# Encoder of two layers on one core: seven up-projection chunks a layer by seven products, with low parts of neighbouring weights made by DMA

## The chip, the core and the metric

The kernel runs on one core of a Trainium2 chip. The core has a matrix engine (TensorE, PE in the profile; PEld are its weight loads), a vector engine (VectorE, DVE), an activation engine (ScalarE, ACT), GpSimd (POOL) and SyncE (SP). Each runs its own stream of instructions in order and waits for the others by semaphores. DMA transfers are issued by one of these engines and then run on 16 DMA engines. The metric is the device time of one execution in microseconds; less is better.

## The reference

What must be computed, for 512 tokens (`S`) of 1024 features (`D_MODEL`), all in float32, for two layers (a gated linear attention mixer in layer 0, softmax attention in layer 1):

```python
for i in range(DEPTH):
    h = rmsnorm(x, norm_mix[i])
    x = x + (gla_mixer(h, ...) if i % 2 == 0 else attn_mixer(h, ...))
    x = x + conv_ffn(rmsnorm(x, norm_ffn[i]), ffn_w_up[i], ffn_w_conv[i], ffn_b_conv[i], ffn_w_down[i])

def conv_ffn(h, w_up, w_conv, b_conv, w_down):
    u = h @ w_up                          # 512 x 1024 by 1024 x 5632
    u = depthwise convolution of width 3 along the tokens, + b_conv
    val, gate = jnp.split(u, 2, axis=-1)
    return (jax.nn.silu(gate) * val) @ w_down     # 512 x 2816 by 2816 x 1024
```

The change concerns `h @ w_up` in both layers.

## The kernel before

**Products of float32.** A float32 matrix is held as a high part (`wh`, rounded to the matrix engine's format fp32r) and a low part (`wl`, what the rounding left). One product is three matmuls: high by high (L361), high by low (L362), low by high (L363).

**Chunks.** The up projection of a layer has 22 chunks m, 0 to 21. A chunk is 128 features of the value and 128 of the gate. A plain chunk (`plain_up`) is two halves t = 0 and 1, each of 8 blocks of 128 input features by three matmuls of 512 columns: 24 matmuls a half, 48 a chunk. The results get the norm's factor in L804 (DVE), then the convolution (`act_up`: L859 on ACT, L860 and L861 on DVE, for each half), the activation (L863, ACT) and the product of the two (L864, DVE). Two finished chunks are made into operands of the down projection by `prepare`, with `split` (L870 ACT, L871 DVE).

**Chunks by seven products.** For a chunk in the list `SEVEN`, `seven_up` multiplies blocks of two by two in the manner of Strassen and Winograd: seven products of sums of blocks in place of eight. Each is 12 matmuls of 256 columns (L816), 84 a chunk. The sums of input blocks are made once a layer, those of weights for every such chunk, by `summed`: L158, L159, L166, L172 add on DVE; the high parts are made on ACT (L162 twice, L174, L183, L187); the low parts on DVE (L163 twice, L175, L188), except the low part of the piece h = 2: there ACT writes minus the high part into the low tile (L184, a copy with scale −1, rounded as the high part is) and a DMA on POOL's queue adds the raw weights to it (L194), which leaves the low part. The piece h = 1 lies in a tile of its own, `ring`, of which there is one. The products come in the order 1, 6, 7, 2, 5, 4, 3. Product 1 is begun between the halves of the chunk before it (the `begun` list). ACT copies partial results between banks (L827 after product 1, L831 after product 6, which product 4 adds to; L841, L842, L845), and DVE finishes them (L836, L843 to L849).

**Down projection.** Right after the first half of chunks 9 and 17 `down_part` begins one of two parts of the down projection, by seven products too, in four rows of outputs; its copies on ACT are L930, L939 and L945. What the parts leave is done plainly at the end of the layer.

**Weights.** A strip is the 1 MB of weights of one chunk, loaded by SP's queue (L136) into `raw`, of which there are two buffers. A buffer is free for the next strip when everything that reads the last one is done: for a plain chunk that is both halves' high and low parts. The halves are split into `wh` and `wl`, three buffers of each. For a plain half that is one copy on ACT (L204) and one subtraction on DVE (L205), both of 1024 elements a partition. Matrices in the list `by_dma` (some of the attention's) are done in the other way: two copies on ACT (L144 into `wh`, L145 negated into `wl`) and the accumulating DMA (L194) on POOL's queue.

**The order.** Nothing plans the order but the program text: `W.todo` lists halves and pieces in the order in which they are used, `W.half` or `W.piece` first issues the DMAs that are pending (`flush`), makes what is asked for if it isn't made, and then makes more from the list until as many are made ahead as its last argument says. That argument is 1 for a plain half and 2 to 5 near a chunk by seven products or a down part, by the table `ahead`; for pieces it is 3.

Of the kernel before, what the change touches and what calls it, by code (L numbers as in the profile page):

```python
# [45 lines left out]
DOWN_AFTER = {9: 0, 17: 1}  # L46


SEVEN = (5, 12, 19, 21)


PC_NORM = 0
# [7 lines left out]
def hybrid_encoder_kernel(  # L60
# [54 lines left out]
    class Weights:  # L115
# [2 lines left out]

        def __init__(self):
            self.todo, self.made, self.raw, self.by_dma, self.pending = [], {}, {}, [], []  # L120
            self.sums, self.last, self.fine = set(), None, []

        def add(self, src, strips=None, pieces=2):
            for i in strips or range(src.shape[0]):
# [4 lines left out]
        def make(self, key):  # L129
            src, i, h = key  # L130
            if h == 0 and (id(src), i) not in self.raw:
                t = sp.tile([P, 4 * S], F32, tag="raw", bufs=2, name=nm("raw"))
                n = 4 if any(src is a and i < m for a, m in self.fine) else 1
                for q in range(n):
                    sl = slice(q * 4 * S // n, (q + 1) * 4 * S // n)
                    sync.dma_start(t[:, sl], src[i, :, sl])  # L136
                self.raw[id(src), i] = t
            if (id(src), i) in self.sums:
                self.made[id(src), i, h] = self.summed(self.raw[id(src), i], h)
                return  # L140
            r = self.raw[id(src), i][:, h * 2 * S : (h + 1) * 2 * S]
            hi, lo = pair("wh", 3, F32R, "wh"), pair("wl", 3, F32R, "wl")
            if any(src is a and i < n for a, n in self.by_dma):
                act.activation(hi, r, AF.Copy)  # L144
                act.activation(lo, r, AF.Copy, scale=-1.0)  # L145
                self.pending.append((lo, r))
            else:
                self.split(hi, lo, r, 2 if src is w_vg and i < 2 else 1, src is w_vg and i == 0 and h == 0)
            self.made[id(src), i, h] = (hi, lo)
# [73 lines left out]
    W = Weights()  # L223
# [8 lines left out]

    def add_ffn(layer):
        first = 0
        for m, part in DOWN_AFTER.items():
            add_up(layer, range(first, m + 1))
            W.add(down_w[layer], range(part * NQ, (part + 1) * NQ), 4)
# [136 lines left out]
    def feature_tile(*a):  # L374
        for last in feature_steps(*a):
            pass
        return last
# [396 lines left out]
    def ffn(layer, norm, cw, nxt):  # L774
# [10 lines left out]
        def plain_up(m):  # L785

            pss = []
            for t in range(2):
                ps = bank("s" if t else "acc", "up")
                feature_tile(*W.half(up[layer], 2 * m + t, ahead.get((m, t), 1)), norm.hl, ps)  # L790
                pss.append(ps)
                if t == 0 and m + 1 in SEVEN:
                    begun.append(seven_up(m + 1))
# [531 lines left out]
```

## Time and profile before

| What | us |
| --- | --- |
| Median of three runs (1109.46, 1110.05, 1112.25) | 1110.05 |
| The profiled execution's own time | 1110.01 |
| Its span | 1108.3 |
| PE busy | 1099.6 (99%) |
| DVE busy | 852.9 (77%) |
| ACT busy | 614.8 (55%) |
| POOL busy | 94.5 (9%) |
| The feed-forward stage of layer 0 within the span | about 225 to 560 |

The profile is of one execution. Busy time of an engine is time in which one of its instructions ran. "Idle before" and the releaser say how long an engine stood still before an instruction and which instruction ended that. Matmuls are pipelined, so the time from start to start says what one costs, and the ends are modelled. Starts are in us from the span's start. The plain chunks of layer 0 fall, for example, into 243.20 to 264.96 (two chunks); the four chunks by seven products end at 291.35, 406.91, 522.89 and 543.87.

### The profile page before, as it was taken

Reading aid. Unit: us, or ns where it says so; the run is one execution under the profiler, and the core shown is the slowest. Engines: PE = TensorE matmul, PEld = TensorE weight load, DVE = VectorE, ACT = ScalarE, POOL = GpSimd, SP = SyncE. Lnnn points to the kernel's source line nnn. Section 1 sums busy time; section 2 is a strip of 40 time slices with the busy share of each in tenths; the row PEclk is TensorE's granted clock in tenths of the full one; section 3 lists DMA queues with packets and bytes.
Section 4 is the critical chain, followed back from the end, with each engine's and each line's share of the span. In section 5 each row is a group of like instructions: output and inputs, shape, how many; then the busy total and the mean of one; then the engine's idle time right before and its main releaser. Section 6 shows DMA issues by size and latency. Waiting matters only on the chain.

```text
span 1108.3 us, 15700 instructions
## 1 busy us (share of the span) xinstructions
PE 1099.6 (99%) x6068; PEld 956.3 (86%) x6068; DVE 852.9 (77%) x1401; ACT 614.8 (55%) x998; POOL 94.5 (9%) x102
## 2 busy tenths in 40 slices
PE   9999999999999999999999999999999999999998
PEld 7888888888889988898888888788888998889887
DVE  6785785679998878976965578766999887897693
ACT  5565343456656554654664777645665655465460
POOL 0100122000000000000004243000000000000000
PEclk9999999999999999999999999999999999999999
DMA  6422222222426343353447765422151634335342
GB/s 231 141 88 97 75 96 76 77 77 92 156 67 179 98 133 114 107 160 95 145 139 187 173 182 154 161 77 81 72 171 47 179 118 133 114 98 156 109 134 76
DMA packets 32571, 134.78 MB, mean 122 GB/s; under 512 B 3952, under 2 KB 4464, under 8 KB 22128
## 3 DMA queue, kind: packets, MB, share of 16 engines
q1 hardware_dynamic: 21072, 102.16, 26.5%
q0 software_dynamic: 6528, 23.07, 10.6%
q10 hardware_dynamic: 4896, 8.55, 2.1%
q8 instruction: 47, 0.77, 0.3%
q14 instruction: 28, 0.23, 0.1%
HBM read 100.21 MB, written 2.10 MB: 92 GB/s over the span
## 4 chain that ended last, share of the span: by engine, by line
PE 93%; DVE 4%; ACT 1%; DMA 1%; issue 0%; POOL 0%; ACTq 0%; SPq 0%; DVEq 0%
PE r L816 21%; PE up L361 11%; PE up L362 11%; PE up L363 11%; PE vg L393 8%; PE op L419 8%; PE dn L362 2%; PE dn L363 2%; PE dn L361 2%; PE o L687 1%; PE A L361 1%; PE av L393 1%; PE A L363 1%; PE A L362 1%; PE pt L1184 1%; PE q L361 1%
## 5 line engine op out<-in xcount | busy, mean ns | idle before, releaser
L361 PE MATMUL up<-xhl,wh 128*128 128x512 f32 x576 | 224.8, 390 | 0.0
L362 PE MATMUL up<-xhl,wh 128*128 128x512 f32 x576 | 224.4, 390 | 0.0
L363 PE MATMUL up<-xhl,wl 128*128 128x512 f32 x576 | 224.2, 389 | 0.0
L204 ACT ACTIVATE wh<-raw 128x1024 fp32r<-128x1024 f32 x116 | 122.6, 1057 | 142.2 <-PE up L362 58.4
L205 DVE TENSOR_TENSOR wl<-raw,wh 128x1024 fp32r<-128x1024 f32 x116 | 141.5, 1220 | 31.7 <-ACT wh L204 31.4
L363 PEld LDWEIGHTS up<-xhl,wl 128*128 128x128 f32 x576 | 108.1, 188 | 22.6
L361 PEld LDWEIGHTS up<-xhl,wh 128*128 128x128 f32 x576 | 108.2, 188 | 21.8
L362 PEld LDWEIGHTS up<-xhl,wh 128*128 128x128 f32 x576 | 108.2, 188 | 21.6
L816 PE MATMUL r<-gu,wh 128*128 128x256 f32 x640 | 116.6, 283 | 0.6 <-ACT r L945 0.6
L816 PEld LDWEIGHTS r<-gu,wh 128*128 128x128 f32 x640 | 99.7, 191 | 1.3 <-ACT r L945 1.0
L194 POOL DMA_DIRECT2D wl<-raw x40 | 35.4, 885 | 683.1 <-ACT r L930 173.7
L859 ACT ACTIVATE y<-u,cw 128x512 f32<-128x512 f32 x88 | 69.2, 808 | 39.2 <-DVE u L804 25.6
L816 PE MATMUL r<-gu,wl 128*128 128x256 f32 x320 | 90.4, 283 | 0.0
L393 PE MATMUL vg<-wh,xhl 128*128 128x512 f32 x256 | 80.1, 392 | 0.4 <-DVE wh L202 0.4
L419 PE MATMUL op<-oT,wh 128*128 128x512 f32 x256 | 71.9, 395 | 0.6 <-ACT p L1148 0.6
L860 DVE SCALAR_TENSOR_TENSOR y<-u,cw,y 128x511 f32<-128x511 f32 x88 | 64.4, 746 | 9.9 <-ACT y L859 9.8
L804 DVE TENSOR_TENSOR u<-up,R 128x512 f32<-128x512 f32 x72 | 48.6, 685 | 26.1 <-PE up L363 25.8
L861 DVE SCALAR_TENSOR_TENSOR y<-u,cw,y 128x511 f32<-128x511 f32 x88 | 64.2, 746 | 0.7
L816 PEld LDWEIGHTS r<-gu,wl 128*128 128x128 f32 x320 | 61.1, 191 | 0.0
L863 ACT ACTIVATE y<-y 128x512 f32<-128x512 f32 x44 | 27.7, 629 | 53.9 <-DVE y L861 53.9
L393 PEld LDWEIGHTS vg<-wh,xhl 128*128 128x128 f32 x256 | 48.3, 189 | 10.6 <-ACT sq L335 0.7
L419 PEld LDWEIGHTS op<-oT,wh 128*128 128x128 f32 x256 | 47.3, 188 | 11.1 <-ACT p L1148 0.9
(264 smaller groups left out, 2325.9 us busy)
## 6 DMA issues: line engine op xcount, KB each, us to landing
raw<-in_w_up_dram SPq DMA_DIRECT2D x42, 1024.0 KB, 4.8
raw<-in_w_down_dram SPq DMA_DIRECT2D x22, 1024.0 KB, 4.9
wl<-raw POOLq DMA_DIRECT2D x40, 512.0 KB, 4.6
raw<-in_w_vg_dram SPq DMA_DIRECT2D x6, 1024.0 KB, 4.8
ring<-p ACTq DMA_DIRECT2D x22, 256.0 KB, 2.8
raw<-in_w_kq_dram SPq DMA_DIRECT2D x4, 1024.0 KB, 4.9
raw<-in_w_gout_dram SPq DMA_DIRECT2D x4, 1024.0 KB, 4.8
raw<-in_w_aout_dram SPq DMA_DIRECT2D x16, 256.0 KB, 4.9
```

The source lines that it names most:

```text
L204: act.activation(hi[:, sl], r[:, sl], AF.Copy)
L205: dve.tensor_tensor(lo[:, sl], r[:, sl], hi[:, sl].bitcast(F32), ALU.subtract)
L361: mm(ps, wh, mh, start=start, stop=False)
L362: mm(ps, wh, ml, start=False, stop=False)
L363: return mm(ps, wl, mh, start=False, stop=stop)
L393: mm(ps[j][:, :width], hl[k][i == 2][:, j * P : (j + 1) * P], (wl if i == 1 else wh)[:, sl], start=k == 0 and i == 0, stop=k == KC - 1 and ...
L419: mm(pss[ng][n], wt[:, sl], mv, start=k == 0 and i == 0, stop=k == KC - 1 and i == 2)
L804: dve.tensor_tensor(u, ps, norm.R, ALU.mult)
L816: mm(dst, w[:, sl], m, start=start and j == 0 and a == 0, stop=j == len(pairs) - 1 and a == 2, skip_group_check=True)
L859: act.activation(y, u, AF.Identity, scale=w(1), bias=w(3))
L860: dve.scalar_tensor_tensor(y[:, 1:], u[:, : S - 1], w(0), y[:, 1:], ALU.mult, ALU.add)
L861: dve.scalar_tensor_tensor(y[:, : S - 1], u[:, 1:], w(2), y[:, : S - 1], ALU.mult, ALU.add)
```

## The change

The list `SEVEN` grows from 4 to 7 chunks a layer. The lists and orders that are derived from it follow: which strips are summed, where product 1 is begun, the table `ahead`. Beside it, three halves for each chunk m of the list get their low part by DMA, as `by_dma` does it, where these halves are plain: the first half of chunk m − 1 and both halves of chunk m + 1. These are (4,0), (10,0), (18,0) and both halves of 6, 8, 12, 14, 16 and 20: 15 a layer. Last, a plain half is asked for with two made ahead by default, no longer one.

```diff
-SEVEN = (5, 12, 19, 21)
+SEVEN = (5, 7, 11, 13, 15, 19, 21)
...
         def __init__(self):
             self.todo, self.made, self.raw, self.by_dma, self.pending = [], {}, {}, [], []
-            self.sums, self.last, self.fine = set(), None, []
+            self.sums, self.last, self.fine, self.joined = set(), None, [], set()
...
             hi, lo = pair("wh", 3, F32R, "wh"), pair("wl", 3, F32R, "wl")
-            if any(src is a and i < n for a, n in self.by_dma):
+            if any(src is a and i < n for a, n in self.by_dma) or (id(src), i, h) in self.joined:
                 act.activation(hi, r, AF.Copy)
                 act.activation(lo, r, AF.Copy, scale=-1.0)
                 self.pending.append((lo, r))
...
     def add_ffn(layer):
         first = 0
+        W.joined |= {(id(up[layer]), m + d, t) for m in SEVEN for d, t in ((-1, 0), (1, 0), (1, 1))}
         for m, part in DOWN_AFTER.items():
...
-                feature_tile(*W.half(up[layer], 2 * m + t, ahead.get((m, t), 1)), norm.hl, ps)
+                feature_tile(*W.half(up[layer], 2 * m + t, ahead.get((m, t), 2)), norm.hl, ps)
```

From line 235 on the lines of the kernel after are one higher: its L805 is L804 here.

In the order of instructions the number of rows goes from 1399 to 1429 on DVE, from 986 to 1070 on ACT, from 99 to 135 on POOL. Three places show what happens. The first is ACT around chunk 14 of layer 0, a plain chunk. Before, its second half and the first of chunk 15 are one copy each, among the convolutions of the chunks (`u` is a chunk's result, `y` the convolution's):

```order
L204 ACTIVATE wh_3856<-raw_3738 128x1024
L859 ACTIVATE y_3826<-u_3824,cw 128x512
L863 ACTIVATE y_3768<-y_3768 128x512
L204 ACTIVATE wh_3887<-raw_3885 128x1024
L859 ACTIVATE y_3832<-u_3830,cw 128x512
L863 ACTIVATE y_3832<-y_3832 128x512
```

After, chunk 14 (`raw_3833`) lies between 13 and 15, which are by seven products. `r` are the banks of 13, `raw_3839` is the strip of 15:

```order
L144 ACTIVATE wh_3835<-raw_3833 128x1024
L145 ACTIVATE wl_3836<-raw_3833 128x1024
L832 ACTIVATE r_3901<-r_3824 128x256
L162 ACTIVATE wh_3844<-raw_3839 128x512
L860 ACTIVATE y_3877<-u_3875,cw 128x512
L162 ACTIVATE wh_3844<-sum_3841 128x512
L860 ACTIVATE y_3883<-u_3881,cw 128x512
L144 ACTIVATE wh_3956<-raw_3833 128x1024
L145 ACTIVATE wl_3957<-raw_3833 128x1024
```

Each half now takes two copies, and the copy L832 of chunk 13 (L831 before) stands behind the first two; L162 of the next strip stands behind that.

The second place is DVE there. Before:

```order
L205 TENSOR_TENSOR wl_3857<-raw_3738,wh_3856 128x1024
L864 TENSOR_TENSOR y_3763<-y_3763,y_3768 128x512
L804 TENSOR_TENSOR u_3830<-up_3799,R_2073 128x512
L205 TENSOR_TENSOR wl_3888<-raw_3885,wh_3887 128x1024
L860 SCALAR_TENSOR_TENSOR y_3832<-u_3830,cw,y_3832 128x511
L861 SCALAR_TENSOR_TENSOR y_3832<-u_3830,cw,y_3832 128x511
```

After, with the sums of chunk 15's strip:

```order
L805 TENSOR_TENSOR u_3881<-up_3826,R_2077 128x512
L158 TENSOR_TENSOR sum_3841<-raw_3839 128x512
L163 TENSOR_TENSOR wl_3845<-raw_3839,wh_3844 128x512
L159 TENSOR_TENSOR raw_3839<-raw_3839 128x512
L861 SCALAR_TENSOR_TENSOR y_3877<-u_3875,cw,y_3877 128x511
L163 TENSOR_TENSOR wl_3845<-sum_3841,wh_3844 128x512
L862 SCALAR_TENSOR_TENSOR y_3877<-u_3875,cw,y_3877 128x511
```

No L205 is left at this place; the sums and low parts of the next strip stand in its stead.

The third place is ACT at the last output row of the first down part, where the strip of chunk 10 is first split. Before:

```order
L945 ACTIVATE r_3300<-r_3210 128x256
L204 ACTIVATE wh_3359<-raw_3357 128x1024
L930 ACTIVATE r_3333<-r_3315 128x256
L174 ACTIVATE wh_3340<-sum_3338 128x512
L939 ACTIVATE r_3375<-r_3333 128x256
```

After, where the strip of chunk 11 (`raw_3460`) is by seven products:

```order
L946 ACTIVATE r_3369<-r_3279 128x256
L144 ACTIVATE wh_3428<-raw_3426 128x1024
L145 ACTIVATE wl_3429<-raw_3426 128x1024
L931 ACTIVATE r_3402<-r_3384 128x256
L174 ACTIVATE wh_3409<-sum_3407 128x512
L940 ACTIVATE r_3445<-r_3402 128x256
L871 ACTIVATE gu_3534<-y_3039 128x512
L162 ACTIVATE wh_3465<-raw_3460 128x512
L162 ACTIVATE wh_3465<-sum_3462 128x512
L946 ACTIVATE r_3495<-r_3402 128x256
```

The copy L930 (now L931) stands behind one more copy, and the last copy L945 (now L946) behind the two L162 of a strip.

## The prediction

> **What bounds the kernel now.** I read the page's busy times and chain first:
>
> ```profile
> PE 1099.6 (99%) x6068; PEld 956.3 (86%) x6068; DVE 852.9 (77%) x1401; ACT 614.8 (55%) x998; POOL 94.5 (9%) x102
> PEclk9999999999999999999999999999999999999999
> PE 93%; DVE 4%; ACT 1%; DMA 1%; issue 0%; POOL 0%; ACTq 0%; SPq 0%; DVEq 0%
> ```
>
> The matrix engine works for 99% of the span at full clock, and 93% of the chain that ended last is its own. So only fewer or shorter matmuls, or fewer pauses between them, can shorten the kernel; other work can only lengthen it. Next, the busy times by stage: four stretches of one plain chunk and one by seven products each, one of two plain chunks, and the whole feed-forward stage of layer 0 (columns: stretch, length, then busy time of each engine with its instructions).
>
> ```profile
> core 0: us, PE busy (x) PEld busy (x) DVE busy (x) ACT busy (x) POOL busy (x), PEclk, DMA share, GB/s
> 270.40:291.35 20.95, 20.95 (x133) 19.05 (x132) 20.93 (x38) 15.24 (x24) 0.95 (x1) 1.00 0.49 141
> 385.96:406.91 20.95, 20.95 (x133) 19.05 (x132) 14.81 (x23) 11.79 (x18) 0.87 (x1) 1.00 0.52 160
> 501.91:522.89 20.98, 20.98 (x135) 19.06 (x134) 11.69 (x18) 8.91 (x13) 0.87 (x1) 1.00 0.42 126
> 522.89:543.87 20.98, 20.98 (x135) 19.06 (x134) 20.91 (x34) 14.47 (x24) 0.87 (x1) 1.00 0.45 132
> 243.20:264.96 21.76, 21.76 (x97) 18.02 (x96) 21.73 (x41) 15.28 (x24) 0.00 (x0) 1.00 0.20 60
> 225.00:560.00 335.00, 334.83 (x1959) 297.67 (x1958) 283.18 (x457) 191.27 (x288) 11.59 (x13) 1.00 0.39 120
> ```
>
> A mixed pair takes 20.95 to 20.98, two plain chunks 21.76. DVE is full in some of these stretches, busy for 85% of the stage (283.18 of 335.00); ACT for 57%.
>
> **Term 1, the products: −4.7.** A chunk turned into seven products saves 21.76 − 20.97 = 0.79 on PE. Three more in each of two layers make 6 × 0.79 = 4.7. A plain chunk is thus 10.88 and one by seven products 10.09, 0.120 a matmul of its 84. The Trainium skill (TensorE: Matmul & The Clock Gate, back-to-back gaps) gives 2.5 ns over the columns' time for a warm matmul; worked out from that, an estimate, a chunk would go from 10.35 to 9.18, and six would save 7.1. The windows show the smaller saving, so the measured one is taken.
>
> **Term 2, the load of DVE and ACT: 0.** These rows (feed-forward stage of layer 0, busy time and mean ns behind the bar) price what is moved:
>
> ```profile
> L204 ACT ACTIVATE wh<-raw 128x1024 fp32r<-128x1024 f32 x39 | 41.2, 1057 | 36.7 <-PE up L362 29.5 <-PE r L816 2.7 <-PE dn L362 2.7
> L205 DVE TENSOR_TENSOR wl<-raw,wh 128x1024 fp32r<-128x1024 f32 x39 | 47.6, 1220 | 4.3 <-ACT wh L204 4.3
> L188 DVE TENSOR_TENSOR ring<-raw,ring 128x1024 fp32r<-128x1024 f32 x12 | 14.6, 1220 | 5.2 <-ACT ring L187 5.2
> L158 DVE TENSOR_TENSOR sum<-raw 128x512 f32<-128x512 f32 x12 | 8.2, 687 | 4.6 <-DMA raw<-in_w_up_dram 4.5
> L804 DVE TENSOR_TENSOR u<-up,R 128x512 f32<-128x512 f32 x36 | 24.3, 685 | 13.1 <-PE up L363 12.9
> L843 DVE TENSOR_TENSOR u<-u,r 128x256 f32<-128x256 f32 x4 | 1.7, 414 | 0.0
> L184 ACT ACTIVATE wl<-raw 128x1024 fp32r<-128x1024 f32 x12 | 12.5, 1044 | 0.0
> L162 ACT ACTIVATE wh<-sum 128x512 fp32r<-128x512 f32 x12 | 7.6, 629 | 7.6 <-PE up L362 7.0
> L842 ACT ACTIVATE u<-r 128x256 f32<-128x256 f32 x4 | 1.5, 370 | 0.0
> ```
>
> On DVE a chunk by seven products has seven operations like L158 (4.8), L188 (1.2), five like L843 (2.1) and one of 512 columns (0.7), 8.8; a plain one has two L205 and two L804, 3.8. Three chunks add 15.0 a layer, the 15 low parts leave 15 × 1.22 = 18.3: DVE gets 3.3 lighter. ACT gets 15 copies like L184 (15.7) and, for each of three chunks, two L162 and L174 (1.9), L183, L184, L187 (3.1) and five like L842 (1.9) less two L204 (6.9 − 2.1 = 4.8), together 30: 191 + 30 of 335, or 66%. POOL issues 18 more L194 (15 lows, 3 pieces) at 0.87, 16 us of an idle engine. No engine becomes the bound by its sum; a mixed pair keeps some 19 of 20.97 on DVE. PE is the cover, and it is gone only where one piece comes late.
>
> Below nothing: in layer 1 the ring's low part comes late once, in chunk 5; the row says by how much the weight load waited.
>
> ```profile
>   PEld r L816: 0.3, 1
> ```
>
> That is the listing of L188 with who waited for it. L205 of (4,0) no longer stands ahead of it, so this 0.3 goes. **Term 3: −0.3.**
>
> **Term 4, copies held up at the down part: +0.4.** Where a down part ends and the next strip but one is by seven products, this happens today (layer 1, chunks 17 to 19; start, duration, operation, idle time before):
>
> ```profile
> 1026.81 0.64 ACT L162 ACTIVATE wh<-raw 128x512 fp32r<-128x512 f32 x1 [3.01 <-DMA raw<-in_w_up_dram]
> 1027.46 0.63 ACT L162 ACTIVATE wh<-sum 128x512 fp32r<-128x512 f32 x1
> 1027.99 0.37 ACT L945 ACTIVATE r<-r 128x256 f32<-128x256 f32 x1
> ...
> 1027.70 0.28 PE L816 MATMUL r<-gu,wl 128*128 128x256 f32 x1
> 1028.41 0.51 PE L816 MATMUL r<-gu,wh 128*128 128x256 f32 x2 [0.44 <-ACT r L945]
> ```
>
> ACT waits for the strip of chunk 19, the copy L945 is queued behind L162, and PE pauses: 0.71 from start to start where 0.12 is usual, 0.6 lost. The order shows the same sequence for chunks 9, 10, 11 after the change, at two new places. They cost 0 to 0.7 each; by the order the strip's buffer comes free about a microsecond earlier there, so I take 0.2, nearer to none. The other end of this part has a nearer call:
>
> ```profile
> 363.67 1.06 ACT L204 ACTIVATE wh<-raw 128x1024 fp32r<-128x1024 f32 x1
> 365.23 0.37 ACT L930 ACTIVATE r<-r 128x256 f32<-128x256 f32 x1 [0.50 <-PE r L816]
> 366.47 1.59 PE L816 MATMUL r<-gu,ring 128*128 128x256 f32 x12
> ```
>
> Two copies in place of one end at 363.67 + 2.11 = 365.78; L930 then ends at 366.15, before its reader at 366.47. Nothing, by 0.3.
>
> **Term 5, low parts that come late: +1.0.** How long the two DMAs take from issue to landing (least, median, most): L194 in the feed-forward of layer 0, in the attention stage (560 to 760), and the strip loads in the feed-forward:
>
> ```profile
> DMA to landing us min/median/max: 4.5/4.5/5.7
> ...
> DMA to landing us min/median/max: 4.5/5.2/8.6
> ...
> DMA to landing us min/median/max: 4.7/4.8/6.7
> ```
>
> Call E the start of product 6 of a chunk m by seven products. Six products of 12 matmuls take 72 × 0.120 = 8.6, so the first half of m + 1 starts at E + 8.6 and needs its low part at its third matmul, E + 9.05. The order puts L144 where its buffer comes free, at about E. Two copies end at E + 2.1, the DMA lands at E + 6.6: 2.4 to spare. The second half needs its own at E + 15.9 (one half of 5.44, product 1 of the next chunk, 1.4). Its L144 comes at E + 7.2, it lands at E + 13.8: 2.1 to spare. Only then is the strip's buffer free. How this loop of buffer and load looks today, between chunks 19 and 21:
>
> ```profile
> 509.68 0.87 POOL L194 DMA_DIRECT2D wl<-raw  x1 [20.63 <-ACT r L827]
> 514.35 0.33 SPq L136 DMA_DIRECT2D raw<-in_w_up_dram  x1
> 519.21 0.69 DVE L158 TENSOR_TENSOR sum<-raw 128x512 f32<-128x512 f32 x1 [2.60 <-DMA raw<-in_w_up_dram]
> ```
>
> An accumulating DMA, 4.67 later the load, 4.86 later the sums, for which DVE stood still 2.60: the loop of a strip by seven products, with the work of DVE between, comes to about 21.3, against 20.97 of PE. One pair has room for that. Where such pairs follow one another (chunks 11 to 16), lateness adds up, some 0.3 a pair from the loop. ACT has its 15.24 of the fullest pair and two copies more to do, some 17.3 of 20.97, and in the order the splits of `prepare` (three like L162, one like L842, 2.3) stand right ahead of L144 for chunks 14 and 16, where that of chunk 12 has none. So I put L144 at E + 1.4 in the second pair and E + 2.3 in the third; there the low part lands at E + 8.9 and the room is gone, and I count 0.4 lost. ACT's queue also holds the copy L831, needed by product 4 at E + 4.3, behind the two copies: free by 2.2 at first, by little in the third pair. A load beside the accumulation makes it 5.7, 1.2 more, now and then. Bounds: 0 if all keep their median; 1 us at each of some five places a layer, 10 in all, if each DMA takes its longest of the stage. The median is the nearest row: 0.4 a layer for the third pair and 0.1 for chunks 5 to 9, 1.0 for both layers.
>
> Sum: −4.7 − 0.3 + 0.4 + 1.0 = −3.6. The profiled execution took 1110.01, the median is 1110.05: forecast **1106.4**.
>
> **Rivals.** *Late low parts eat the gain.* The same terms with 0.3 to 1 us at most of ten places, since the room of 2.1 to 2.4 is less than the DMAs' spread (5.7 and 6.7 against medians of 4.5 and 4.8 are 3.1 together). The loop's 21.3 speaks for it, the slack of the first pair against. At 0.4 at ten places, 4 us in all in place of the 1.0: 1109.4.
>
> *Slower: accumulation as slow as in the attention stage.* There 8.6 was reached, with more loads in flight. Now 15 more such DMAs a layer run beside strip loads. From a landing of 6.9 on (4.5 + 2.4) every half waits; at 8.6 each of the five first halves a layer is 1.7 late and each strip's load 4 later; 1.7 at ten places is 17, −4.6 + 17 gives 1122. It is a loss from about 0.5 at each of ten places. The 4.5 in full DVE stretches speaks against. The Trainium skill (SBUF — State Buffer, separate sides) has a rule of this direction: a DMA from GpSimd's queue starves when VectorE holds the port that both share, since GpSimd can't write descriptors. The trace disagrees here:
>
> ```profile
> L194 POOL DMA_DIRECT2D wl<-raw x40: 862/872/1086, 278.1 to 1061.3; - x40
> ```
>
> All 40 issues took 862 to 1086 ns, whether DVE was full or not.
>
> *More than forecast.* No new pause, and the old one at L945 gone with its like in layer 0: −4.7 − 0.3 − 2 × 0.5 = −6.0, 1104.0.
>
> *The products don't get shorter* (weight loads of 84 matmuls bind): excluded, PEld is 19.05 of 20.95 in these pairs and the pairs are shorter.
>
> **Numbers.** A measurement of this kernel tells 0.3% (3.3 us) from no change: faster is below 1106.7, slower above 1113.4. The forecast's case, 1104.0 to 1106.7: 0.55, the best case in it. Late parts, 1106.7 to 1113.4: 0.28. Slower, 1113.4 to 1125: 0.17. The range 1104.0 to 1113.4 leaves out the last.
>
> **What would show it.** A mixed pair at 20.95 to 21.0 from chunk 4 to 16; no L205 between these; L194 at 4.5 to 5.7; pauses of PE below 0.5 before L363 of the first halves of 14 and 16, and one at L946 of chunk 9. Wrong if pauses before L363 or behind L832 exceed 1 us in each pair, or if L194 passes 6.9.

## The result: slower by 2.25%

| | before | after |
| --- | --- | --- |
| Median, us (4 runs each) | 1110.94 | 1136.35 |
| Lowest to highest, us | 1109.46 to 1112.25 | 1133.88 to 1136.88 |
| Span of the profiled execution, us | 1108.3 | 1132.2 |

The ratio is 1.0225, 95% interval 1.0203 to 1.0246. The forecast was 1106.4 us, in a range of 1104.0 to 1113.4: wrong in sign and far outside the range. The page of the profile after, its busy times, the granted clock, the chain, the costliest group, and the two DMA groups of the feed-forward with their median time to landing:

```profile
PE 1103.9 (98%) x6284; PEld 963.2 (85%) x6284; DVE 841.6 (74%) x1431; ACT 663.0 (59%) x1082; POOL 125.8 (11%) x138
PEclk9999999999999999999999999999999999999999
PE 51%; DVE 15%; issue 15%; DMA 14%; ACT 4%; POOL 1%; ACTq 0%; SPq 0%; POOLq 0%; DVEq 0%
L364 PE MATMUL up<-xhl,wl 128*128 128x512 f32 x480 | 189.5, 395 | 13.4 <-DMA wl<-raw 12.3
raw<-in_w_up_dram SPq DMA_DIRECT2D x42, 1024.0 KB, 5.0
wl<-raw POOLq DMA_DIRECT2D x76, 512.0 KB, 5.1
```

PE's own share of the chain (the work that ended last, followed back) fell from 93% to 51%; DMA has 14% of it. L364 is the matmul that reads the low part of a weight (L363 before): PE stood idle ahead of it for 13.4 us, 12.3 of these until an accumulating DMA landed.

Where the time went is told by the up stages, from the first matmul of the up projection to the first of the plain down projection, of both layers. Before:

```profile
225.46:543.87 318.41, 318.24 (x1886) 283.96 (x1885) 270.90 (x439) 183.12 (x276) 11.59 (x13) 1.00 0.39 118
752.90:1071.91 319.01, 318.49 (x1885) 283.98 (x1884) 271.04 (x439) 184.41 (x277) 11.44 (x13) 1.00 0.38 117
```

After, with three stretches of one plain chunk and one by seven products ahead of them:

```profile
380.20:401.18 20.98, 20.98 (x134) 19.06 (x133) 9.01 (x18) 7.71 (x11) 1.75 (x2) 1.00 0.53 139
401.18:425.47 24.29, 21.53 (x135) 19.04 (x134) 21.00 (x37) 17.81 (x29) 2.62 (x3) 1.00 0.65 162
425.47:448.06 22.59, 21.52 (x135) 19.05 (x133) 20.82 (x39) 19.04 (x30) 3.49 (x4) 1.00 0.63 163
225.73:556.75 331.02, 319.66 (x1993) 286.87 (x1992) 265.22 (x454) 207.33 (x318) 27.32 (x31) 1.00 0.53 142
764.89:1095.81 330.92, 320.92 (x1994) 287.82 (x1993) 265.20 (x454) 208.59 (x319) 27.00 (x31) 0.99 0.53 142
```

The stages are 12.6 and 11.9 us longer, together 24.5, and the span grew by 23.9; the rest of the kernel is as it was. The pair 380.20 to 401.18 takes the 20.98 that was forecast. The next two take 24.29 and 22.59, with PE busy for 21.5 of each and DVE for 21.0 and 20.8, so neither engine is full there.

How much of this is pauses was worked out from the starts of all matmuls in these stages: what the time from one start to the next has above 0.2267 us (512 columns) or 0.1193 us (256 columns), summed where it is over 0.05. At these two rates all matmuls of the stage add up to 317.55 us before and 314.97 after, so by the rates the products save 2.58 a layer, 0.86 for each chunk. (The stages less their pauses are 317.8 and 315.6, which is 2.2 a layer.) The pauses, of both layers, in us, by the matmul that waited:

| Matmul that waited | before | after |
| --- | --- | --- |
| low part of a plain half (L363, now L364) | 0.0 | 16.2 |
| product of an up chunk by seven | 0.4 | 4.6 |
| product of a down part | 1.1 | 6.8 |
| others | 0.4 | 3.1 |
| sum | 1.8 | 30.7 |

28.9 more pause less 5.2 of products is 23.7; the 0.8 that is left of the stages' 24.5 are pauses under 0.05 each. Not all of the 30.7 is waiting: at the end of the longest pause of layer 1 (2.64, until 942.43) the granted clock falls to 0.5 for 3.4 us, matmuls of 512 columns start 0.43 apart, and 1.6 us are lost by that. The columns are those of the stages above, the granted clock is the third number from the end:

```profile
942.20:945.60 3.40, 3.17 (x8) 2.49 (x9) 3.40 (x7) 2.50 (x5) 0.86 (x1) 0.50 0.10 19
```

In some of the runs below this counts for more, and is given there. One of the pauses in full, the largest of layer 0 (the load of a strip, an accumulation, PE; start, duration, operation, idle time before):

```profile
394.61 0.33 SPq L136 DMA_DIRECT2D raw<-in_w_up_dram  x1
...
394.89 0.87 POOL L194 DMA_DIRECT2D wl<-raw  x1 [4.11 <-ACT r L832]
...
401.41 0.40 PE L363 MATMUL up<-xhl,wh 128*128 128x512 f32 x1
404.16 0.50 PE L364 MATMUL up<-xhl,wl 128*128 128x512 f32 x1 [2.35 <-DMA wl<-raw]
```

The load of the strip of chunk 13 and the accumulation for the first half of chunk 12 are issued within 0.28 us. The listing of L194 and that of L136, each narrowed to this one transfer, give their times from issue to landing:

```profile
DMA to landing us min/median/max: 9.2/9.2/9.2
...
DMA to landing us min/median/max: 6.5/6.5/6.5
```

9.2 in place of 4.5 and 6.5 in place of 4.9. The accumulation was issued 2.3 after the start of product 6 (392.57), lands at 404.1, and PE, which would have wanted it at 401.64, waits 2.5. Why the two start together is seen from the buffers: the strip of 13 waits for the buffer of 11, which comes free when the accumulation for a piece of 11 lands (issued at 389.91, landed 4.6 later, 394.5); and ACT is done with the copies for (12,0) at 394.6.

Over seven of the kernels of this study (the kernel after and the runs ahead_one, copies_stay, no_half_before, not_ten_eighteen, piece_on_dve and spaced), the time from issue to landing in the up stages by how long after the accumulation the strip load was issued (accumulations with one load from 6 us before to 5 after and no other accumulation within 5, worked out from the traces; in the first row the accumulation has landed before the load is issued):

```
load issued, us after     accumulation, us        strip load, us
the accumulation     n    median (least to most)  median (least to most)
 4 to 5             61    4.54 (4.49 to 4.59)     4.95 (4.70 to 6.40)
 0 to 1              5    9.08 (6.91 to 9.98)     6.73 (6.39 to 7.39)
-1 to 0             10    7.84 (6.70 to 8.94)     6.15 (5.06 to 7.00)
-2 to -1            47    6.17 (5.58 to 8.12)     5.17 (4.82 to 6.77)
-3 to -2            17    5.36 (4.79 to 6.22)     4.95 (4.77 to 5.97)
-4 to -3            25    5.19 (4.53 to 6.40)     4.90 (4.70 to 5.26)
```

Issued within a microsecond of each other, the accumulation takes 7.8 to 9.1 in the median, where both one after the other would take 4.54 + 4.95 = 9.5, and the load suffers too. The traces' records of single DMA packets (128 of 8 KB for a load, 128 of 4 KB for an accumulation) show that one does run after the other. A load's first packet starts 0.96 to 1.01 us after its issue in all of these cases but one, an accumulation's some 1.43 after its own when nothing is in the way. So a load that is issued up to some 0.4 us later still comes first. In the pair above its packets run from 395.56 to 400.79; those of the accumulation start at 399.76, 4.9 us after its issue, and end at 403.81. In the 13 cases of the table in which the load was issued from 1 us before the accumulation to 0.3 us after it, at most one of the accumulation's 128 packets starts before 90% of the load's have. Only the load issued 0.74 later found the accumulation under way.

VectorE can't be what held the accumulation back in this pair. DVE stood still from 393.5 until the strip had landed:

```profile
401.17 0.69 DVE L158 TENSOR_TENSOR sum<-raw 128x512 f32<-128x512 f32 x1 [7.70 <-DMA raw<-in_w_up_dram]
```

### The profile page after: what moved, and what is told of

It reads as the page before. It is cut to its first block, busy times and chain, and to the rows that moved or that the text cites. A ratio compares the mean times of both kernels' runs of the same rounds, so it can differ in the third digit from the quotient of the medians.

```text
span 1132.2 us, 16421 instructions
## 1 busy us (share of the span) xinstructions
PE 1103.9 (98%) x6284; PEld 963.2 (85%) x6284; DVE 841.6 (74%) x1431; ACT 663.0 (59%) x1082; POOL 125.8 (11%) x138
## 4 chain that ended last, share of the span: by engine, by line
PE 51%; DVE 15%; issue 15%; DMA 14%; ACT 4%; POOL 1%; ACTq 0%; SPq 0%; POOLq 0%; DVEq 0%
PE vg L394 8%; PE op L420 8%; PE r L817 7%; DMA wl<-raw 6%; DMA raw<-in_w_up_dram 5%; DVE y L861 2%; DVE y L862 2%; DMA raw<-in_w_down_dram 2%; PE up L364 2%; PE dn L362 2%; PE dn L363 2%; PE dn L364 2%; PE up L362 2%; PE up L363 2%; DVE wl L205 1%
## 5 line engine op out<-in xcount | busy, mean ns | idle before, releaser
L364 PE MATMUL up<-xhl,wl 128*128 128x512 f32 x480 | 189.5, 395 | 13.4 <-DMA wl<-raw 12.3
L362 PE MATMUL up<-xhl,wh 128*128 128x512 f32 x480 | 188.2, 392 | 0.0
L363 PE MATMUL up<-xhl,wh 128*128 128x512 f32 x480 | 187.7, 391 | 0.0
L194 POOL DMA_DIRECT2D wl<-raw x76 | 66.9, 880 | 676.8 <-ACT r L828 118.3
L204 ACT ACTIVATE wh<-raw 128x1024 fp32r<-128x1024 f32 x74 | 78.1, 1055 | 98.3 <-PE op L420 32.2
L364 PEld LDWEIGHTS up<-xhl,wl 128*128 128x128 f32 x480 | 90.5, 188 | 38.7 <-DMA wl<-raw 17.2
L205 DVE TENSOR_TENSOR wl<-raw,wh 128x1024 fp32r<-128x1024 f32 x74 | 90.3, 1220 | 27.6 <-ACT wh L204 27.4
L363 PEld LDWEIGHTS up<-xhl,wh 128*128 128x128 f32 x480 | 90.6, 189 | 17.8
L362 PEld LDWEIGHTS up<-xhl,wh 128*128 128x128 f32 x480 | 90.7, 189 | 17.0
L860 ACT ACTIVATE y<-u,cw 128x512 f32<-128x512 f32 x88 | 69.2, 808 | 45.8 <-DVE u L805 24.5
L861 DVE SCALAR_TENSOR_TENSOR y<-u,cw,y 128x511 f32<-128x511 f32 x88 | 64.3, 745 | 12.4 <-ACT y L860 12.3
L144 ACT ACTIVATE wh<-raw 128x1024 fp32r<-128x1024 f32 x46 | 48.4, 1051 | 30.6 <-PE up L363 9.3
L817 PE MATMUL r<-xhl,wh 128*128 128x256 f32 x336 | 62.3, 283 | 0.0
L162 ACT ACTIVATE wh<-raw 128x512 fp32r<-128x512 f32 x30 | 18.9, 631 | 73.7 <-DMA raw<-in_w_up_dram 43.6
L158 DVE TENSOR_TENSOR sum<-raw 128x512 f32<-128x512 f32 x30 | 20.6, 687 | 51.0 <-DMA raw<-in_w_up_dram 51.0
```

Of the source, the lines that this page charges most:

```text
L194: pool.dma_start(lo.bitcast(F32), r, accum_op=ALU.add)
L204: act.activation(hi[:, sl], r[:, sl], AF.Copy)
L205: dve.tensor_tensor(lo[:, sl], r[:, sl], hi[:, sl].bitcast(F32), ALU.subtract)
L362: mm(ps, wh, mh, start=start, stop=False)
L363: mm(ps, wh, ml, start=False, stop=False)
L364: return mm(ps, wl, mh, start=False, stop=stop)
```

## The experiments

Three theories. A: the pauses come from accumulations that meet strip loads. B: they come from the second copy on ACT, which holds up what is queued behind it. C: DVE can't carry seven such chunks, however the low parts are made. A fourth, D, came after the first runs: one loop that is too long. Edits are against the kernel after, where nothing else is said; ratios are to the kernel before, with 95% intervals. Pauses are summed as above.

**Only the list grows** (run sevens_only). The low parts stay on DVE, one half ahead:

```diff
-        W.joined |= {(id(up[layer]), m + d, t) for m in SEVEN for d, t in ((-1, 0), (1, 0), (1, 1))}
+        W.joined |= set()
...
-                feature_tile(*W.half(up[layer], 2 * m + t, ahead.get((m, t), 2)), norm.hl, ps)
+                feature_tile(*W.half(up[layer], 2 * m + t, ahead.get((m, t), 1)), norm.hl, ps)
```

> Only the list of seven chunks grows; all low parts of plain halves by L205 on DVE again, one half made ahead. Theory A (the pauses come from accumulating DMAs that queue behind strip loads on the 16 DMA engines): those pauses go; what is left is DVE, which in a pair of chunks would have some 19 + 3 x 1.22 = 22.7 us to do in 20.97, 1.7 us over in about four pairs a layer, so -4.7 + up to 13: 1106 to 1119, and L194 lands in 4.5 to 5.7 us at all its pieces. Theory B (the second copy on ACT holds up what is queued behind it): no second copies, about 1106 to 1108. Theory C (DVE can't carry seven such chunks, in whatever way the low parts are made): 1130 or more, as after the change or worse.

Measured: 1123.42, ratio 1.0114 (1.0091 to 1.0137). Between A's upper end and C, far above B. The pauses are 20.2 us here, and they are others; who waited for whom on PE in the up stage of layer 0 (us in total, times, longest):

```profile
PE r L817 <- DMA wl<-raw: 2.6, 3, 1.3
PE r L817 <- DVE ring L188: 1.4, 1, 1.4
PE r L817 <- ACT r L832: 1.3, 1, 1.3
PE up L364 <- DVE wl L205: 1.2, 1, 1.2
```

So seven chunks without relief for DVE do cost, and more than the 13 us that its rows in a pair (22.7 to do in 20.97) gave. The waits are mixed, and the largest group is again for accumulations, those of the pieces h = 2 of chunks and down parts; no run takes the 20.2 apart. The change's remedy costs still more than the ill: the kernel after is 13 us slower than this, and with the same one half ahead it is 27 us slower (next run). Seven chunks without the DMA and with two ahead weren't run.

**One half ahead again** (run ahead_one).

```diff
-                feature_tile(*W.half(up[layer], 2 * m + t, ahead.get((m, t), 2)), norm.hl, ps)
+                feature_tile(*W.half(up[layer], 2 * m + t, ahead.get((m, t), 1)), norm.hl, ps)
```

> As changed, but plain halves again one ahead by default. Theory A: the copies of the second halves come later, so their accumulations meet other loads; the first halves after a seven chunk are set by the table and still meet the strip load: pauses of 2 us before L364 stay, 1130 to 1150. Theory B: as after the change, 1134 to 1138. If making two ahead was what brought the transfers together: below 1125.

Measured: 1150.75, ratio 1.0353 (1.0321 to 1.0384). As A expected, at its upper end: PE's waits at L364 for accumulations are 12.3 us in layer 0 alone, up to 5.1 each. Of its 46 us of pauses 8.9 are matmuls at a granted clock of 0.5, in five stretches of 3.4 or 6.8 us, each next to a pause of 2.5 to 5.3. With one ahead the DMA way is 14 us slower than with two.

**The old list with the DMA** (run old_list_joined).

```diff
-SEVEN = (5, 7, 11, 13, 15, 19, 21)
+SEVEN = (5, 12, 19, 21)
```

> The old list of four chunks, low parts of its neighbours by DMA, two ahead. Theory A: the first halves of chunks 6, 13 and 20 and the first half of 18 meet strip loads, 0.7 to 2.6 us each, in both layers: 1110 + 2 x (3 x 1.5 + 1.4) = 1122, with landings of L194 of 6 to 9.5 us there. Theory B: 0.6 to 1 us at each of the three copies L832 a layer behind two copies: 1112 to 1115. Theory C: no more chunks and less work on DVE: 1109 to 1110.

Measured: 1116.21, ratio 1.0053 (1.0034 to 1.0072), between A and B. It has no more chunks than before and less work on DVE, and is slower by 5.9: C is out as the sole cause. In the profiled executions, whose spans differ by 6.2, the up stages have 3.5 of this; 2.7 lie between them, in the attention stage, where the granted clock was 0.5 from 634.2 to 641.0. Of the pauses most is at the copy L946, 2.0 and 1.7 us in the two layers where the kernel before has 0.3 and 0.6; at L364 only 0.4 and 0.3. A's 0.7 to 2.6 for each first half was too much: the accumulations for the first halves of 6, 13 and 20 are issued 1.6 to 2.4 us behind a load and land in 5.0 to 6.0, not in the 6 to 9.5 that A put.

**The copies stay, the transfer goes** (run copies_stay). For the first half after a chunk by seven products both ACT copies stay, and DVE then overwrites the low part:

```diff
-                self.pending.append((lo, r))
+                if any(src is a for a in up) and h == 0 and i - 1 in SEVEN:
+                    dve.tensor_tensor(lo, r, hi.bitcast(F32), ALU.subtract)
+                else:
+                    self.pending.append((lo, r))
```

> As changed, but for the first half of chunk m + 1 both copies on ACT stay as they are and the low part is then overwritten by DVE (a subtraction of 1.22 us) in place of the accumulating DMA: same load of ACT, less DMA, more DVE (6 of these a layer, 7.3 us). Theory A: the pauses before L364 of these halves (7.5 us in layer 0, about 15 in both) mostly go, 1 to 3 come back from DVE: 1121 to 1126, and the second halves' accumulations land as before. Theory B: they stay, 1133 to 1138. Theory C: longer than after the change, above 1138.

Measured: 1120.54, ratio 1.0092 (1.007 to 1.0115): 16 us less than after the change, with ACT's load unchanged and DVE's raised. That decides against B for these waits; the result is just below A's range. PE's waits in the up stage of layer 0 (the lines of this kernel are three higher: L367 is L364, L949 is L946, L835 is L832):

```profile
PE r L820 <- ACT r L949: 3.5, 2, 2.2
PE r L820 <- ACT r L835: 1.7, 3, 0.8
PE up L367 <- DMA wl<-raw: 0.4, 1, 0.4
PE r L820 <- DMA wl<-raw: 0.3, 1, 0.3
```

Against these, the same view of the kernel after:

```profile
PE up L364 <- DMA wl<-raw: 5.9, 5, 2.4
PE r L817 <- ACT r L946: 3.2, 2, 1.6
PE r L817 <- ACT r L832: 1.1, 2, 0.7
```

The waits for accumulations at L364 went from 5.9 to 0.4 (L367 here). Those at L946 stayed; they are the next question.

**The half before stays on DVE** (run no_half_before). Only (1, 0) and (1, 1) are left in the set, which takes (4,0), (10,0) and (18,0) out:

```diff
-        W.joined |= {(id(up[layer]), m + d, t) for m in SEVEN for d, t in ((-1, 0), (1, 0), (1, 1))}
+        W.joined |= {(id(up[layer]), m + d, t) for m in SEVEN for d, t in ((1, 0), (1, 1))}
```

> As changed, but the first half of the chunk before a seven chunk keeps its low part on DVE where it isn't also the first half after one: (4,0), (10,0) and (18,0). Theory A says that the DMA of (10,0) and (18,0) slows the load of the strip of 11 and 19 to 7.3 us, and that L162 waits for this and L946 behind it: these four pauses of 1.35 to 1.8 us fall to the 0.3 to 0.6 of before, -4 to -6: 1130 to 1132. Were they due to the second copy ahead of L931, the same; were they due to the list alone, 1135 to 1137.

Measured: 1136.62, ratio 1.0238 (1.021 to 1.0266): nothing gained. Yet the pauses at L946 are gone. Others had grown, most of all at the first halves of 6 and 8 (3.1 and 5.3 us in layer 1, where the kernel after has 0.5 and 1.3). Three of the long waits are next to stretches at a granted clock of 0.5, which cost 5.7 of this run's 34.1 us of pauses, against 1.6 of 30.7 after the change. Why the others grew was left open here and tested below.

**Second halves only** (run second_half_only).

```diff
-        W.joined |= {(id(up[layer]), m + d, t) for m in SEVEN for d, t in ((-1, 0), (1, 0), (1, 1))}
+        W.joined |= {(id(up[layer]), m + d, t) for m in SEVEN for d, t in ((1, 1),)}
```

> As changed, but only the second half of the chunk after a seven chunk gets its low part by DMA; all first halves by L205. DVE is 9 x 1.22 = 11 us a layer heavier than after the change, in a pair 20.2 of 20.97. Theory A: pauses before L364 of first halves and at L946 go (some 21 us in both layers): 1136 - 21 + 0 to 4 from DVE: 1115 to 1119. Theory C (DVE is the bound once a pair is nearly full): 1122 or more, near the 1123 without any of these DMAs.

Measured: 1119.67, ratio 1.0071 (1.0056 to 1.0086), just above A's range and below C's. 17 us less than after the change, with the pauses at low parts of plain halves down to 6.6 us in both layers, those of the down parts to 4.4.

**The same with another order on ACT** (run second_half_copy_earlier; the edit of the last run holds too). One less made ahead at the half before a chunk by seven products:

```diff
-        ahead.update({(m - 1 + i // 2, i % 2): n for m in SEVEN for i, n in ((-1, 2), (0, 2), (1, 5))})
+        ahead.update({(m - 1 + i // 2, i % 2): n for m in SEVEN for i, n in ((-1, 2), (0, 2), (1, 4))})
...
-                pieces[h] = W.piece(src, strip, h, 3)
+                pieces[h] = W.piece(src, strip, h, 2 if i == 6 and pairs is inputs else 3)
...
             act.activation(r3, r2, AF.Copy)
+            W.ahead(1)
```

> As the run with second halves only, with the order on ACT changed: four, not five, made ahead at the half before, so that the copies of the next first half and of the next strip stand later against the copies after products 1 and 6. Theory B (ACT's order makes the pauses of 0.6 to 1.1 us that end on the copy after product 6, some 4 us in both layers): 3 us shorter than that run; else the same within 1.5 us.

Measured: 1117.95 (1115.26 to 1118.95), ratio 1.0055 (1.0036 to 1.0073). 1.7 less than the last run, with intervals that overlap: inconclusive for B at the copy L832.

**Theory D: a loop** (run piece_on_dve). The strip of one seven chunk can be loaded when the piece of the last is accumulated; that needs its copies, which on ACT stand behind DVE's work on its sums and outputs; and those begin when its strip has landed. To shorten this loop, the piece h = 2 of up chunks gets its low part on DVE; the 15 halves keep the DMA:

```diff
...
-            if h == 2:
+            if h == 2 and not own:
                 act.activation(hi, r, AF.Copy)
                 act.activation(lo, r, AF.Copy, scale=-1.0)
...
```

(`own` is an argument that `summed` gets; it is true for strips of the up projection.)

> As changed, but the low part of the piece h = 2 of every up chunk by seven products is made by DVE (1.22 us) in place of a second copy on ACT and an accumulating DMA; the 15 halves a layer stay with the DMA. A new theory D: from one strip of a seven chunk to the next goes a loop (load about 5 us, 8.7 of DVE's work on its sums and on the chunk's outputs, 3.8 of ACT's until the second copy of the piece, accumulation 4.5, then the buffer is free), 22 us and more against 20.97 of PE, and every pause is this loop's lag coming out at one wait or another. It gets 4 us shorter here, so most pauses go: 1112 to 1118. Theory A alone (each pause is one collision of an accumulation with a strip load): the first halves still meet loads, 1127 to 1134.

Measured: 1129.35, ratio 1.017 (1.0152 to 1.0188). A's range, not D's. Of its 27.2 us of pauses 6.2 are matmuls at a granted clock of 0.5, next to pauses of 2.2 to 3.2. What the run shows is finer: in chunks 11 to 16 of layer 0 the loads and accumulations now miss each other, all landing in 4.5 to 4.7, and of the 5.8 us of pauses that the kernel after has there 0.6 is left; in chunk 6 they still meet (accumulation issued at 285.54, load at 286.28). The strip of 7 then lands at 293.0, after the change at 290.2; ACT waits for it in L162, the copies for (6,1) behind that come 2.9 later, and 3.2 us are lost at (6,1) and 1.3 at (8,0), whose accumulation takes only 4.6 but is issued late. The landings of L194, from 390 to 440, and of the one at 285.54:

```profile
DMA to landing us min/median/max: 4.5/4.6/4.7
...
DMA to landing us min/median/max: 6.9/6.9/6.9
```

**Chunks further apart** (run spaced).

```diff
-SEVEN = (5, 7, 11, 13, 15, 19, 21)
+SEVEN = (5, 8, 12, 15, 21)
```

> As changed with the list (5, 8, 12, 15, 21): five chunks, at least three apart, 13 halves a layer by DMA, two ahead. Products: 2 x 0.79 = 1.6 less than before. Theory D: the loop has 31 us and more from strip to strip, so lag doesn't add up: 1109 to 1113. Theory A alone: the first half after each of these chunks still waits 0.6 to 2.5 us, four a layer: 1115 to 1122.

Measured: 1126.43, ratio 1.0145 (1.0123 to 1.0167): above both ranges, and far above D's. The worst pause, 3.8 us in chunk 9 of layer 0, stands behind an accumulation that was issued 0.1 us before a load (319.50 and 319.60) and took 10.0 to land. Of its 20.1 us of pauses 3.0 are matmuls at a granted clock of 0.5, next to this one. With distance between the chunks there is no lag to add up, and the meeting alone does it. D falls as the cause of all pauses. That a loop with little room turns a late transfer into a late next one isn't excluded by these runs.

**Two ahead alone** (run ahead_two_alone), in the kernel before:

```diff
-                feature_tile(*W.half(up[layer], 2 * m + t, ahead.get((m, t), 1)), norm.hl, ps)
+                feature_tile(*W.half(up[layer], 2 * m + t, ahead.get((m, t), 2)), norm.hl, ps)
```

> The kernel before with plain halves two ahead by default, nothing else. All theories: no change beyond 2 us, 1109 to 1112; DVE does the same work, a little earlier.

Measured: 1110.41, ratio 1.0007 (0.9993 to 1.002). No change, as expected: with the old list and nothing by DMA, this part of the change is free.

**(10,0) and (18,0) on DVE, (4,0) by DMA** (run not_ten_eighteen; its L365 is L364 of the kernel after). The question that was left open:

```diff
         W.joined |= {(id(up[layer]), m + d, t) for m in SEVEN for d, t in ((-1, 0), (1, 0), (1, 1))}
+        W.joined -= {(id(up[layer]), m, 0) for m in (10, 18)}
```

> As changed, but (10,0) and (18,0) alone keep their low part on DVE; (4,0) stays with the DMA, unlike in the run no_half_before. If the four pauses at L946 come from these two halves' transfers beside the strip loads of 11 and 19, and that run gave the gain back only because (4,0) on DVE shifted the transfers of chunks 6 and 8 into the loads: the pauses at L946 fall from 6.4 us to about 1.5 and those of chunks 5 to 9 stay as after the change, 1130 to 1132. If a pause that is taken away comes back elsewhere whatever one does (a loop that is too long): 1135 to 1137.

Measured: 1126.99, ratio 1.0145 (1.0126 to 1.0164), 9.4 less than after the change and more than expected. The pauses of the down parts fall from 6.8 to 0.8 us, and those at (6,0) and (8,0) of layer 1 are back at 0.4 and 1.1. So the gain of the run no_half_before had been lost in chunks 4 to 9. There the accumulation for (6,0) was issued 0.5 before a load, after the change 1.6 behind it (the issues of no_half_before first, then those after the change):

```profile
285.95 0.88 POOL L194 DMA_DIRECT2D wl<-raw  x1 [6.96 <-ACT wl L145]
...
286.46 0.33 SPq L136 DMA_DIRECT2D raw<-in_w_up_dram  x1
```

```profile
284.96 0.33 SPq L136 DMA_DIRECT2D raw<-in_w_up_dram  x1
...
286.56 0.86 POOL L194 DMA_DIRECT2D wl<-raw  x1 [5.44 <-ACT r L832]
```

The accumulation took 8.5 us in the first and 6.1 in the second, the load 7.4 and 5.2: a shift of 2 us between two queues made both over 2 us slower. In the traces the up stages are 6.6 us shorter than after the change, and the down parts have 6.0 of that. The medians differ by 9.4, the two profiled executions by only 5.0: the one of the kernel after is the fastest of its four, the one here is nearly the slowest. So what the 9.4 has beyond that isn't shown by the traces.

**More chunks without the DMA** (run one_more_chunk). If the transfers are the ill, more products should pay where DVE has room, without them. From the kernel before:

```diff
-SEVEN = (5, 12, 19, 21)
+SEVEN = (5, 12, 15, 19, 21)
```

> The kernel before with chunk 15 added to its list, nothing by DMA, one ahead. The products save 2 x 0.79 = 1.6. DVE gets 5.0 us more in a stretch of four plain chunks that has 5.6 idle. If the idle time there is free for it: 1108.5 to 1109.5. If DVE's work comes in the wrong order, pauses at the ring's low part L188 or at L363: 1111 to 1115.

Measured: 1110.33, ratio 0.9997 (0.9982 to 1.0011). Layer 0 has no pause above 0.25 us, layer 1 one of 2.0, in chunk 21, at the accumulated piece:

```profile
PE r L816 <- DMA wl<-raw: 1.9, 1, 1.9
```

Its transfer was issued at 1060.60, 24.5 us after that of chunk 19, and took 5.7. That would be D's loop at work, in one place. The next run (five_own_piece) tests it, with the piece of chunk 19 alone on DVE, as in the run piece_on_dve but for this strip; against the run one_more_chunk:

```diff
-                self.made[id(src), i, h] = self.summed(self.raw[id(src), i], h)
+                self.made[id(src), i, h] = self.summed(self.raw[id(src), i], h, i == 19 and any(src is a for a in up))
...
-            if h == 2:
+            if h == 2 and not own:
```

> The run one_more_chunk (list 5, 12, 15, 19, 21, nothing by DMA) with the low part of the piece h = 2 of chunk 19 alone made by DVE, so that the strip of 21 is loaded some 4 us earlier. That run had one pause of 2.0 us in layer 1, at this piece of chunk 21, and none above 0.25 us in layer 0. If its loop of accumulation and load was the cause, the pause goes: 1107.5 to 1109, 0.1 to 0.3% under the kernel before. If DVE, full in these two chunks, is late by the 1.2 us more instead: 1110 to 1112.

Measured: 1106.07 (1105.86 to 1108.61), ratio 0.9961 (0.9948 to 0.9975) to the kernel before. The pause is gone, and this version beats both. Its up stages, and PE's busy time in them:

```profile
225.34:542.55 317.21, 317.21 (x1922) 284.92 (x1921) 277.43 (x453) 186.85 (x284) 11.57 (x13) 1.00 0.39 120
750.41:1067.91 317.50, 317.47 (x1922) 284.96 (x1921) 277.49 (x453) 188.24 (x285) 11.42 (x13) 1.00 0.39 120
```

No pause above 0.25 us is left. The two up stages are 2.7 us shorter than those of the kernel before: 1.7 by products, the rest by pauses, of which those at L945 are gone too; no run tests the cause of that. The profiled spans differ by 4.0. The other 1.3 lie outside the up stages, mostly between them (209.0 before, 207.9 here), and aren't explained. Part of the 4.3 us by the ratio goes with the clock: all six executions here had a mean granted clock of 1.000, seven of the eleven of the kernel before had 0.997 or 0.998, and the other four have a median of 1109.0, 2.9 above this run's. Whether the edit or chance brought that, no run shows. DVE is busy for 277 us of 317 without being late.

**Six chunks** (run six_chunks), a version between: the order of the run second_half_copy_earlier with

```diff
-SEVEN = (5, 7, 11, 13, 15, 19, 21)
+SEVEN = (5, 11, 13, 15, 19, 21)
...
-        W.joined |= {(id(up[layer]), m + d, t) for m in SEVEN for d, t in ((1, 1),)}
+        W.joined |= {(id(up[layer]), m, 1) for m in (12, 14, 16)}
```

> A version drawn from the runs: the order of the run second_half_copy_earlier, six chunks (5, 11, 13, 15, 19, 21), and by DMA only the second halves of 12, 14 and 16. Products 4 x 0.79 = 3.2 less than before. The pauses of that run between chunks 5 and 9 (some 3 us a layer) go with chunk 7, those of 0.4 to 1.2 around 14 and 21 stay: 1107 to 1111 by theory D. By theory A the same, since its accumulations there landed without touching L364.

Measured: 1111.93, ratio 1.0012 (0.9999 to 1.0025): no gain, and just above the 1107 to 1111 that both theories gave. 8.0 us of pauses are left, 3.2 of them at plain halves that wait for DVE or for an accumulation.

## Why the prediction was wrong

**Term 1 (products, −4.7) was right**: by the rates of the matmuls it is 5.2, by the stages less their pauses 4.3.

**Term 2 (load of DVE and ACT, 0) was right as a sum and misleading.** DVE went from 270.9 to 265.2 in layer 0's up stage (forecast −3.3), ACT from 183 to 207 (+24; forecast +30), POOL from 11.6 to 27.3 (+16, as forecast). No engine is full. The sentence that PE is the cover except where one piece comes late was true too, but there were some twenty such places. Nor did the sum have room for a clock that falls: it took full clock from the profile before, and beside long pauses the granted clock was 0.5.

**Term 3 (the ring, −0.3)**: no wait for L188 is left. Right, and too small to matter.

**Term 4 (down parts, +0.4) failed.** Measured: +5.7 (1.1 to 6.8). The strip was forecast to come a microsecond earlier than its like; it came about a microsecond later, and PE lost 1.3 to 1.8 at four places, the two that were there before among them. After the change, ACT and PE at chunks 9 to 11 of layer 0:

```profile
377.07 0.63 ACT L162 ACTIVATE wh<-raw 128x512 fp32r<-128x512 f32 x1 [4.63 <-PE r L817]
...
378.25 0.37 ACT L946 ACTIVATE r<-r 128x256 f32<-128x256 f32 x1
...
378.67 0.50 PE L817 MATMUL r<-gu,wh 128*128 128x256 f32 x2 [1.53 <-ACT r L946]
```

The load was issued at 369.70, the accumulation for (10,0) at 369.33; they took 7.3 and 9.5. The view names a matmul as what ended ACT's wait, but the strip landed at 376.96, just before, and at two of the other three places the view names this load. The queueing of L946 behind L162 was foreseen; that the half (10,0) itself slows the strip which L162 waits for was not. The run not_ten_eighteen shows it: without the transfers for (10,0) and (18,0) 0.8 of the 6.8 is left.

**Term 5 (late low parts, +1.0) is the step that failed most**: 16.2 at the low parts of plain halves, 4.6 at the products of up chunks. The issues were nearly right: for the first halves of 12, 14 and 16 of layer 0 L194 came at E + 2.3, 4.9 and 4.9, where 2.1, 3.5 and 4.4 follow from what was put. With a landing in 4.54 the last two would be late by 0.3 to 0.4 each. Wrong was above all the landing time. "A load beside the accumulation makes it 5.7, 1.2 more, now and then": the 5.7 is the most of a stage in which the next strip load is issued when an accumulation has landed and the last one was issued over 3.6 us before it, so the two never started together; that row couldn't show the cost of a meeting. The one stage where they do, with its 8.6 (for an accumulation that was issued 0.16 us after a load), was put into a rival. And "now and then" overlooked that the order makes them meet: the landing of one piece's accumulation frees the buffer, and so starts a load, at the time at which ACT finishes the next half.

**The rivals.** *Slower* had the mechanism, a price (1.7 at ten places, 1122) and a turning point, with a chance of 0.17; it should have been the forecast. Its 1122 is still 14 below the 1136 measured: it had 0.4 at the down parts where 5.7 came, five first halves a layer where the change has six, and 8.6 where 9.5 was reached. The landing in the feed-forward is 5.2 in the median and 9.5 at most, as in the attention stage (5.2 and 8.6). The Trainium skill's rule there (SBUF — State Buffer, separate sides), that VectorE keeps GpSimd from writing descriptors, isn't what did it: all 76 issues took 862 to 1087 ns, and in the pair shown above DVE stood still. The Trainium skill (DMA: Bandwidth & Descriptors, queues, rings and completion order) says that each DMA engine takes turns between the queues and drains a whole packet of one before it switches. The trace agrees in that one is drained before the other, but here that is nearly the whole transfer, 5.2 us of the load's packets, and no turns within it are seen; whether this is one packet in the sense of that page, no run here shows.

*Late low parts eat the gain* was of the right kind and far too small. The loop of 21.3 that spoke for it took 23.7 and 23.1 (L194 for the pieces of 11, 13 and 15 at 389.91, 413.65 and 436.78).

**What would show it**: the pair of chunks 10 and 11 has its 20.98, and L205 is gone from the halves concerned. The pauses before the first halves of 14 and 16 were to be below 0.5 and are 0.5 and 1.3, and that of 12, for which none was forecast, is 2.5; and the condition given for being wrong, L194 past 6.9, is the one that came true.

## What to carry to other kernels

Moving work from an engine to a DMA queue is priced by what else the DMA engines do at that moment, not by the transfer's time when alone: look up which transfers the new one will be issued beside, and what starts these. Where the landing of one transfer frees the buffer for the next, the program's own order may bring a third to the same point every time. A pause can also cost more than its own length, when the granted clock falls beside it. A maximum from a stage in which two transfers can't start together is no upper bound; the row to take is from a stage where they do, however far away. And before relieving an engine for seven more expensive chunks, try the one or two that fit into the time it has.

## What the runs showed of the hardware

An accumulating DMA of 512 KB took 4.54 us alone, 6.2 when a 1 MB load had been issued 1 to 2 us before it, 7.8 at under 1 us, and 9.1 when the load came up to 1 us after it; that load then took 6.7 in place of 4.95. So being issued first didn't protect the accumulation: it was the worst case of the table. The load's first packet started 0.96 us after its issue, the accumulation's 1.43 after its own, so a load issued 0.1 to 0.3 us later came first, and the accumulation's packets waited until most of the load's had started. A shift of some 2 us between the two queues decided 2 to 3 us of landing time.

In the up stages of the sixteen traces the granted clock fell to 0.5 for 3.4 or 6.8 us beside every pause of more than 3 us (seven) and beside 7 of the 16 pauses between 2 and 3 us, and nowhere else. Each of these stretches cost 1.5 to 3.0 us on top of the pause.
